# Unscaled tokens into the experts, and two modulation units moved ahead of them

## The chip, the core and the metric

The kernel runs on one core of one Trainium2 chip. The metric is the device time of one execution in microseconds; times of a kernel are given as the median of its runs. Engines are called by the profile's names: PE (TensorE, matrix products and transposes; PEld is its weight load), DVE (VectorE), ACT (ScalarE), POOL (GpSimd), SP (SyncE, which issues almost all DMAs; SPq is its queue).

## What is computed

256 tokens of width 1024 pass a first block and then two layers of a second block. The change touches the first block's mixture of experts and the second block's modulation:

```
x  = x + merged @ w_out                                  # first block, after attention and gMLP
h2 = rms_norm(x, norm2_g)                                # one scale per token, one gain per channel
gp = softmax(h2 @ rg_w + rg_b);  top-1 group of 4        # router
el = (h2 @ re_w + re_b) of that group's 8 experts; softmax, top-2, weights renormalised
y  = sum over 32 experts:  comb[:, e] * ((silu(h2 @ w_gate[e]) * (h2 @ w_up[e])) @ w_down[e])
x  = rms_norm(x + y, final_norm_g)
...
mod = silu(c) @ w_ada[l] + b_ada[l]                      # second block, for each layer l: shift, scale, gate
h   = rms_norm(x) * (1 + scale) + shift; RG-LRU and mLSTM branches; x = x + gate * (mix @ w_out_2[l])
```

All values are float32. Where a product needs precision, an operand is split into a high part rounded to the fp32r type and the remainder (`...h` and `...l` in the names), and three products replace one.

## The kernel before

Tokens lie in two tiles of 128 partitions (`i` = 0, 1), `x1[:, i, :]` with 1024 columns. The stretch that the change works on starts with the output projection of the first block, `out_proj` (L820), called at L960 with the four accumulators (token tile i, column half n); the last one, (1, 1), is cut in two pieces of 256 columns. Its last steps run accumulator by accumulator. Each finished accumulator goes to `fin1` (L939): DVE adds it to `x1` (L943), ACT squares it for the norm (`token_scale` L336, `meansq` L365), and POOL makes the norm scale `r2[:, i, 3:4]` (L373) once a token tile is complete.

The router follows: `r_transpose` (L892) transposes x1 on PE and copies it to `h2T` on DVE (L898), `r_logits` (L900) multiplies it with the router weights, `r_choice` (L909) is a chain of small DVE operations that ends in the mask `M` (L923) of each token's two experts, and `r_place` (L927) counts slots with a product of `M` and a triangle (L932). The dictionary `late` hangs the router's work for token tile 0 and the first half of tile 1 in front of steps of the projection. `r_tokens` (L884) makes the experts' input: ACT reads x1 with a step of eight columns, scales it by `r2`, and writes the high part `h2h` (L888); a second such ACT pass (L889) writes the scaled value in full, and DVE takes the difference `h2l` (L890).

Experts work in 16 pairs with 64 slots an expert. `Slots.half` (L982) builds a one-hot matrix `oht` of tokens against the 256 slots of two pairs on DVE, `gather` (matmuls at L1030) multiplies `h2h` and `h2l` with it, so that the slots' inputs `xg` come out transposed. A test of whether any expert has over 64 tokens (L1053, L1054) branches to a general path, which does not run with these inputs. `spread` (L242) copies token values along the partitions through a diagonal matrix made on POOL (L250) and a product (L252), into `bc` (L1103). For each pair, DVE picks each slot's weight out of `bc` (L1152), PE multiplies with gate and up weights (L1165), ACT takes the silu (L1169), DVE multiplies (L1170), and one pair later `down` (L1109) and `back` (L1128) apply the down weights and return the slots to the tokens. `eloads` (L486) issues the experts' weight chunks on SP's queue (1 MB of gate and up, or 1 MB of down), in a fixed order and as buffers come free.

A modulation unit, `ada_unit` (L393), loads 2 MB of `w_ada` as two tiles, multiplies them with silu(c) (L401, 16 rows of the profile for one unit), has ACT copy the result (L403) and later folds it into a column form (`ada_fold` L414, eight matmul rows at L421 for one unit, then DVE at L423 and L425). Layer 1's units (1, 0) to (1, 3) carry its shift and scale. Before the change (1, 0) stands at the start of the second block (L1275), and (1, 1), (1, 2) and (1, 3) are taken from the list `units` during layer 0's last part (L1559).

A scheduler sets the order of instructions on each engine, from the order written and a table of costs. `tc.keep_in_program_order` pins an instruction to its place among the pinned, and `tc.issue_after` forces an order behind another instruction. `warm` (L350) issues products whose result nobody reads.

## Time and profile before

| | before |
|---|---|
| median of 3 runs | 967.88 us (967.02 to 968.38) |
| profiled execution | 967.82 us, span 966.0 us |
| mean granted TensorE clock | 0.972 |
| PE busy | 908.2 us, 94% of the span |
| DVE, ACT, POOL busy | 597.6, 461.9, 22.6 us |

The span runs from the first to the last instruction; 1.8 us of the profiled execution lie outside it. In a timeline row the columns are start, busy time, engine, line, operation, output and inputs, shapes and count, and in brackets how long the engine had been idle before and what released it. A row with a count over 1 stands for several instructions in sequence, and its time runs over all of them. [...]

### The profile page before, as it was taken

To read this page: it belongs to the slowest core of one execution; us is meant where nothing else is said; L and a number is where in the kernel's file an instruction comes from. 1 tells how busy PE (TensorE), PEld (TensorE's weight loads), DVE (VectorE), ACT (ScalarE), POOL (GpSimd) and SP (SyncE) were. 2 spreads that over 40 slices of the span, in tenths; PEclk is the share of its full clock that TensorE was granted. 3 is DMA by queue.
4 is the path that set the end of the run, shared out by engine and by line. 5 is a ranking of instruction groups with operands and counts; after the bars stand their busy time and mean duration, and the time that the engine had idled before them with its cause. 6 is when DMAs were issued, how large, how long until landed. Compare 5 with 4: busy or idle time off the path is not lost.

```text
span 966.0 us, 15088 instructions
## 1 busy us (share of the span) xinstructions
PE 908.2 (94%) x5936; PEld 702.5 (73%) x5936; DVE 597.6 (62%) x1157; ACT 461.9 (48%) x806; POOL 22.6 (2%) x40
## 2 busy tenths in 40 slices
PE   7929998998899999999999999999999999999997
PEld 5928986997444445545448998897787999889776
DVE  5617773484366446445357979446756888935865
ACT  4513564353422112222136778565554678755742
POOL 1000000000100000000000000000100000000100
PEclk9968999998899999999999999999999999999999
DMA  9868479862798999999769753754627954574201
GB/s 317 247 116 287 131 238 360 324 221 79 268 356 328 401 400 400 403 399 404 265 226 310 235 175 131 256 180 143 228 88 242 281 187 163 172 264 174 88 1 44
DMA packets 135014, 230.22 MB, mean 238 GB/s; under 512 B 5784, under 2 KB 79512, under 8 KB 134936
## 3 DMA queue, kind: packets, MB, share of 16 engines
q1 hardware_dynamic: 132280, 227.00, 68.3%
q10 hardware_dynamic: 2656, 2.17, 0.7%
q8 instruction: 49, 0.80, 0.4%
q14 instruction: 29, 0.24, 0.1%
HBM read 226.53 MB, written 2.62 MB: 237 GB/s over the span
## 4 chain that ended last, share of the span: by engine, by line
PE 61%; DVE 4%; issue 3%; ACT 3%; POOL 1%; POOLq 0%; DVEq 0%; ACTq 0%
PE at L1165 11%; PE mm L272 10%; PE mm L271 10%; PE mm L270 10%; PE mm L1122 6%; PE mm L1135 3%; PE mm L1030 3%; PE mm L401 1%; PE mm L1397 1%; DVE wl L283 1%; PE at L1420 1%; ACT wh L282 1%; PE tp L1430 1%; PE at L271 0%; PE at L270 0%
## 5 line engine op out<-in xcount | busy, mean ns | idle before, releaser
L283 DVE TENSOR_TENSOR wl<-w,wh 128x1024 fp32r<-128x1024 f32 x164 | 199.1, 1218 | 122.1 <-ACT wh L282 120.5
L282 ACT ACTIVATE wh<-w 128x1024 fp32r<-128x1024 f32 x164 | 171.8, 1056 | 138.9 <-PE mm L271 76.4
L270 PE MATMUL mm<-hh,wh 128*128 128x256 f32 (+1 forms) x624 | 179.8, 288 | 3.9 <-ACT wh L282 3.3
L272 PE MATMUL mm<-hh,wl 128*128 128x256 f32 (+1 forms) x624 | 178.9, 288 | 0.8 <-DVE wl L283 0.8
L271 PE MATMUL mm<-hl,wh 128*128 128x256 f32 (+1 forms) x624 | 177.1, 284 | 0.9 <-DVE hl L563 0.9
L270 PEld LDWEIGHTS mm<-hh,wh 128*128 128x128 f32 (+1 forms) x624 | 119.4, 191 | 10.0 <-ACT wh L282 5.1
L1165 PE MATMUL at<-w,xg 128*64 128x512 f32 x512 | 122.9, 595 | 0.2 <-PEq L1054 0.2
L272 PEld LDWEIGHTS mm<-hh,wl 128*128 128x128 f32 (+1 forms) x624 | 119.2, 191 | 3.6 <-issue 1.7
L271 PEld LDWEIGHTS mm<-hl,wh 128*128 128x128 f32 (+1 forms) x624 | 119.2, 191 | 2.9 <-issue 1.5
L1165 PEld LDWEIGHTS at<-w,xg 128*64 128x64 f32 x512 | 38.9, 137 | 70.0 <-issue 65.9
L271 PE MATMUL mm<-wl,hh 128*128 128x256 f32 x256 | 72.1, 283 | 0.0
L272 PE MATMUL mm<-wh,hl 128*128 128x256 f32 x256 | 72.0, 283 | 0.0
L270 PE MATMUL mm<-wh,hh 128*128 128x256 f32 x256 | 71.6, 285 | 0.0
L1122 PE MATMUL mm<-w,heT 128*64 128x512 f32 x256 | 63.2, 598 | 0.0
L271 PEld LDWEIGHTS mm<-wl,hh 128*128 128x128 f32 x256 | 48.4, 189 | 2.7 <-issue 2.4
L270 PEld LDWEIGHTS mm<-wh,hh 128*128 128x128 f32 x256 | 47.6, 188 | 3.7 <-issue 2.0
L272 PEld LDWEIGHTS mm<-wh,hl 128*128 128x128 f32 x256 | 48.3, 189 | 1.7 <-issue 1.5
L1137 DVE TENSOR_TENSOR x<-x,mm 128x512 f32<-128x512 f32 x64 | 40.1, 680 | 14.8 <-PE mm L1135 14.8
L1170 DVE SCALAR_TENSOR_TENSOR sil<-at,wsl,sil 128x256 f32<-128x256 f32 x16 | 7.7, 483 | 66.9 <-ACT sil L1169 66.9
L1124 ACT ACTIVATE ys<-mm 128x512 fp32r<-128x512 f32 x32 | 19.1, 597 | 60.8 <-PE mm L1122 60.8
L1169 ACT ACTIVATE sil<-at 128x256 f32<-128x256 f32 x16 | 6.1, 383 | 79.2 <-PE at L1165 79.2
L1122 PEld LDWEIGHTS mm<-w,heT 128*64 128x64 f32 x256 | 18.7, 136 | 31.5 <-issue 28.7
(436 smaller groups left out, 1772.0 us busy)
## 6 DMA issues: line engine op xcount, KB each, us to landing
w<-in_w_in SPq DMA_DIRECT2D x55, 1024.0 KB, 7.5
w<-in_w_down SPq DMA_DIRECT2D x64, 512.0 KB, 10.3
w<-in_w_gate SPq DMA_DIRECT2D x60, 512.0 KB, 10.3
w<-in_w_up SPq DMA_DIRECT2D x60, 512.0 KB, 10.4
w<-in_w_ada SPq DMA_DIRECT2D x24, 1024.0 KB, 5.2
w<-in_w_out SPq DMA_DIRECT2D x20, 1024.0 KB, 5.0
w<-in_w_gate SPq DMA_DIRECT2D x8, 256.0 KB, 7.6
w<-in_w_up SPq DMA_DIRECT2D x8, 256.0 KB, 7.6
```

Of the source, the lines that this page charges most:

```text
L270: pin(TE.matmul(o, lhsT=lh, rhs=rh, start=start and k == 0, stop=False))
L271: pin(TE.matmul(o, lhsT=lh, rhs=rl, start=False, stop=False))
L272: pin(TE.matmul(o, lhsT=ll, rhs=rh, start=False, stop=stop and k == nk - 1))
L282: splits[S] = S.activation(out=h, in_=src, func=AF.Copy)
L283: splits[V] = V.tensor_tensor(out=l, in0=src, in1=f32(h), op=OP.subtract)
L401: r = TE.matmul(acc[32 * k:32 * k + 32, :], lhsT=cact[:, hf * 4 + k:hf * 4 + k + 1].to_broadcast([P, 32]), rhs=w[:, k * 512:(k + 1) * 512] ...
L1030: TE.matmul(ps[:, 256 * a:256 * a + 256], lhsT=part[i][:, k, :], rhs=oht[:, i, :], start=n == 0, stop=n == 3)
L1122: TE.matmul(po[64 * q:64 * q + 64, :], lhsT=heT[:, f * P + 64 * q:f * P + 64 * q + 64], rhs=wd[n][:, (2 * q + f) * 512:(2 * q + f + 1) * 5 ...
L1124: S.activation(out=y[:, 0, :], in_=po, func=AF.Copy)
L1135: r = TE.matmul(ps, lhsT=ohs[:, i * P:(i + 1) * P], rhs=y[:, part, :], start=part == 0, stop=part == 1)
L1137: V.tensor_tensor(out=xs, in0=xs, in1=ps, op=OP.add)
L1165: r = TE.matmul(gu[64 * q:64 * q + 64, :], lhsT=xg[:, k, o:o + CAP], rhs=w, start=k == 0, stop=k == KT - 1)
```

## The change

Five things change. (a) `r_tokens(i, n)` splits the unscaled x1, half a token tile at a time, right after that half was added: one ACT pass and one DVE subtraction over 512 columns, both reading x1 with a step of eight columns. The scaled copy is gone. (b) The norm scale is applied at the slots: a third `spread` brings `r2` into `bc[:, 4]`, one more DVE operation for each pair sums it over the slot's row into `wsl[:, 2:3]`, and the silu gets it as its scale; the other factor goes into the gate weight `gw`. (c) The units (1, 0) and (1, 1) are loaded while the first block's `w_out` is loaded and multiplied around the last router steps, and folded around the first gather. The later places take (1, 2) and (1, 3). (d) The slot count of token tile 0 is pinned between the accumulators (1, 0) and (1, 1), and four and then six `warm` products are pinned around the slot count of tile 1. (e) The general path's loads go to SP's queue, and no GpSimd DMA scratch is reserved.

```diff
-        def r_tokens(i, pool):
-            h2[i] = pool.tile([P, D], F32, tag=f"y{i}", name=nm("h2"))
...
-            S.activation(out=h2h[i], in_=x1k(i), func=AF.Copy, scale=r2[:, i, 3:4])
-            S.activation(out=h2k, in_=x1k(i), func=AF.Copy, scale=r2[:, i, 3:4])
-            V.tensor_tensor(out=h2l[i], in0=h2k, in1=f32(h2h[i][:]), op=OP.subtract)
+        def r_tokens(i, n):
+            c = slice(64 * n, 64 * n + 64)
+            split(h2h[i][:, :, c], h2l[i][:, :, c], x1k(i)[:, :, c])
...
             if (i, n) == (1, 0):
                 r_choice(0)
-                r_tokens(0, ro)
+            if not i:
+                r_tokens(0, n)
+            if i and n and c == 0:
+                r_tokens(1, 0)
             if i and n and c + w == 512:
-                r_transpose(1, 1)
-                rlast = r_logits(1, 1)
-                r_place(0)
+                pin = tc.keep_in_program_order
+                a = [psum(), psum()]
+                ada_mm(a[0], aws[0][0], 0, pin)
+                r_transpose(1, 1, True)
+                ada_mm(a[0], aws[0][1], 1, pin)
+                rlast = r_logits(1, 1, True)
+                for hf in range(2):
+                    ada_mm(a[1], aws[1][hf], hf, pin)
+                r_choice(1)
+                r_tokens(1, 1)
+                for j in range(2):
+                    ada_end(ro, *nexts.pop(0), a[j])
 
         late = {(6, 0, 1): lambda: [r_transpose(0, n, True) for n in range(2)],
                 (7, 0, 1): lambda: [r_logits(0, n, True) for n in range(2)],
+                (4, 1, 1): lambda: r_place(0, True),
...
+        def between():
+
+            if len(splits_done) == 3:
+                aws.extend(ada_load(*u) for u in nexts[:2])
+            splits_done.append(0)
...
         slots.half(0)
-        warm(6, rlast, h2h[0][:, 0:4, :])
-        r_choice(1)
-        last = r_place(1)
+        warm(4, rlast, h2h[0][:, 0:4, :], True)
+        last = r_place(1, True)
+        warm(6, rlast, h2h[0][:, 0:4, :], True)
...
+            V.tensor_tensor(out=gw, in0=gw, in1=r2[:, :, 3:4], op=OP.mult)
...
-                        G.dma_start(out=wf, in_=w[0, e].rearrange("(p k) c -> p k c", k=KT)[:, 2 * kq:2 * kq + 2, :])
+                        SY.dma_start(out=wf, in_=w[0, e].rearrange("(p k) c -> p k c", k=KT)[:, 2 * kq:2 * kq + 2, :])
...
-        bc = bp.tile([P, 4, T], F32, name="bc")
+        bc = bp.tile([P, 5, T], F32, name="bc")
...
+        pb = psum_t()
+        spread(bp, "sOH", r2[:, :, 3], pb[:, 0:256])
+        S.activation(out=bc[:, 4, :], in_=pb[:, 0:256], func=AF.Copy)
...
+            V.scalar_tensor_tensor(out=oa, in0=f32(ohs[:]), scalar=1.0, in1=bc[:, 4, :], op0=OP.mult, op1=OP.mult, accum_out=wsl[:, 2:3])
...
-            S.activation(out=sil, in_=gu[:, 0:256], func=AF.Silu)
+            S.activation(out=sil, in_=gu[:, 0:256], func=AF.Silu, scale=wsl[:, 2:3])
...
         with tc.issue_after(last.ins):
-            ada_unit(bp, 1, 0)
+            ada_unit(bp, *nexts.pop(0))
...
             if l == 0:
-                units += [(1, 1), (1, 2), (1, 3)]
+                units += nexts
...
-    nc = bacc.Bacc("TRN2", target_bir_lowering=False, num_devices=1)
+    nc = bacc.Bacc("TRN2", target_bir_lowering=False, num_devices=1, dynamic_dma_scratch_size=1024)
```

The order of instructions moves at three places. DVE, around the adds of the projection's results to x1 (`x`, L943 before, L955 after), before:

```order
L943 TENSOR_TENSOR x_66<-x_66,mm_1963 128x512
L943 TENSOR_TENSOR x_66<-x_66,mm_1964 128x512
L340 SCALAR_TENSOR_TENSOR r_1946<-r_1946 128x1
L898 COPY h2T<-tp_2106 128x512
L898 COPY h2T<-tp_2112 128x512
L911 SCALAR_TENSOR_TENSOR lg<-at_2121,r_1946,row_1942 128x36
L890 TENSOR_TENSOR h2l_2151<-h_293_2149,h2h_2150 128x1024
L912 TENSOR_REDUCE gmx_1948<-lg 128x1
L943 TENSOR_TENSOR x_66<-x_66,mm_1965 128x512
```

and with the change:

```order
L955 TENSOR_TENSOR x_66<-x_66,mm_1967 128x512
L283 TENSOR_TENSOR h2l_1965<-x_66,h2h_1963 128x8x64
L955 TENSOR_TENSOR x_66<-x_66,mm_1968 128x512
L340 SCALAR_TENSOR_TENSOR r_1946<-r_1946 128x1
L904 COPY h2T<-tp_2122 128x512
L283 TENSOR_TENSOR h2l_1965<-x_66,h2h_1963 128x8x64
L904 COPY h2T<-tp_2128 128x512
L917 SCALAR_TENSOR_TENSOR lg<-at_2137,r_1946,row_1942 128x36
L918 TENSOR_REDUCE gmx_1948<-lg 128x1
L919 SCALAR_TENSOR_TENSOR gat_1949<-lg,gmx_1948,cst 128x4
L955 TENSOR_TENSOR x_66<-x_66,mm_1969 128x512
```

The one remainder `h2l` of 1024 columns behind the logits has become two of 512 columns, of which one now stands between the two adds of tile 0 and one between the two copies that the logits need.

PE, from the end of the projection to the first gather (`at` takes the last piece, `M` is the mask, `cact` silu(c), `onesr` marks the slot counts' and warm products), before:

```order
L272 MATMUL at_1967<-wo_284_2062,ml 128x256
L895 MATMUL tp_2199<-cst,x_66 128x128 x4
L932 MATMUL at_2209<-M_1957,cst 128x32
L904 MATMUL at_2170<-vec,h2T 128x36 x4
L355 MATMUL tp_2266<-h2h_2150,onesr 128x512 x6
L1046 MATMUL tp_2368<-M_1957,onesr 128x32
L931 MATMUL at_2286<-M_1957,onesr 128x32
L932 MATMUL at_2286<-M_1957,cst 128x32
L1030 MATMUL mm_2316<-oht_2262,h2h_2150 128x256
```

and with the change:

```order
L272 MATMUL at_1971<-wo_284_2066,ml 128x256
L408 MATMUL mm_2218<-w_2072,cact 32x512 x4
L901 MATMUL tp_2224<-cst,x_66 128x128 x4
L408 MATMUL mm_2218<-w_2074,cact 32x512 x4
L910 MATMUL at_2187<-vec,h2T 128x36 x4
L408 MATMUL mm_2219<-w_2076,cact 32x512 x4
L408 MATMUL mm_2219<-w_2078,cact 32x512 x4
L355 MATMUL tp_2310<-h2h_1963,onesr 128x512 x4
L941 MATMUL at_2315<-M_1957,onesr 128x32
L942 MATMUL at_2315<-M_1957,cst 128x32
L355 MATMUL tp_2322<-h2h_1963,onesr 128x512 x6
L1062 MATMUL mm_2352<-oht_2306,h2h_1963 128x256
```

The slot count of tile 0 (`at_2209`) has left this place for one ahead of the last accumulator's products; two modulation units and four warm products have come in, and six warm products stand behind tile 1's slot count.

PE at the end of layer 0's output projection (`tp` and `at` of L1236 are the transposes of the next layer's first token tile, `xn`), before:

```order
L271 MATMUL mm_9641<-wo_9962,mh_9198 128x512
L401 MATMUL mm_9710<-w_9711,cact 32x512 x4
L401 MATMUL mm_9710<-w_9713,cact 32x512 x4
L272 MATMUL mm_9641<-wo_9961,ml_9199 128x512
L270 MATMUL mm_9642<-wh_9955,mh_9198 128x256
L401 MATMUL mm_9771<-w_9772,cact 32x512 x4
L401 MATMUL mm_9771<-w_9774,cact 32x512 x4
L271 MATMUL mm_9642<-wl_9956,mh_9198 128x256
L272 MATMUL mm_9642<-wh_9955,ml_9199 128x256
L421 MATMUL tp_9785<-cst,ada_9709 128x1 x4
L421 MATMUL tp_9832<-cst,ada_9770 128x1 x4
L1236 MATMUL tp_10030<-cst,xn_9635 128x128 x4
```

and with the change:

```order
L271 MATMUL mm_9718<-wo_9996,mh_9275 128x512
L272 MATMUL mm_9718<-wo_9995,ml_9276 128x512
L270 MATMUL mm_9719<-wh_9989,mh_9275 128x256
L271 MATMUL mm_9719<-wl_9990,mh_9275 128x256
L272 MATMUL mm_9719<-wh_9989,ml_9276 128x256
L1272 MATMUL tp_10064<-cst,xn_9712 128x128 x4
```

Both units and both folds are gone from this place.

## Rows read from the trace of the kernel before

**Rows 1.** The page: busy time of each engine, and the chain by engine.
```profile
PE 908.2 (94%) x5936; PEld 702.5 (73%) x5936; DVE 597.6 (62%) x1157; ACT 461.9 (48%) x806; POOL 22.6 (2%) x40
...
PE 61%; DVE 4%; issue 3%; ACT 3%; POOL 1%; POOLq 0%; DVEq 0%; ACTq 0%
```
**Rows 2.** Windows of the run: us, busy time (instructions) by engine, PEclk, DMA share, GB/s.
```profile
230.00:237.00 7.00, 6.71 (x30) 6.42 (x31) 3.40 (x15) 1.24 (x4) 0.00 (x0) 0.51 0.00 0
...
240.40:250.60 10.20, 6.65 (x27) 6.10 (x26) 6.78 (x37) 6.09 (x8) 0.00 (x0) 0.50 0.97 349
```
**Rows 3.** Timeline of PE from the projection's end to the first expert.
```profile
226.91 0.28 PE L272 MATMUL mm<-wh,ml 128*128 128x256 f32 x1
...
230.14 1.12 PE L895 MATMUL tp<-cst,x 128*128 128x128 f32 x4 [2.60 <-DVE x L943]
...
238.95 1.08 PE L904 MATMUL at<-vec,h2T 128*128 128x36 f32 x8 [0.64 <-DVE h2T L898]
239.87 2.49 PE L355 MATMUL tp<-h2h,onesr 128*128 128x512 f32 x6
...
246.60 0.64 PE L932 MATMUL at<-M,cst 128*128 128x32 f32 x2 [3.55 <-DVE M L923]
...
252.83 3.65 PE L1165 MATMUL at<-w,xg 128*64 128x512 f32 x16
```
**Rows 4.** Timeline of DVE in the same stretch.
```profile
221.45 0.69 DVE L943 TENSOR_TENSOR x<-x,mm 128x512 f32<-128x512 f32 x1 [2.03 <-PE mm L272]
222.99 0.16 DVE L340 SCALAR_TENSOR_TENSOR r<-r 128x1 f32<-128x1 f32 x1 [0.85 <-ACT jk L365]
...
228.20 1.22 DVE L890 TENSOR_TENSOR h2l<-h,h2h 128x1024 fp32r<-128x1024 f32 x1 [1.78 <-ACT h L889]
...
237.25 0.42 DVE L943 TENSOR_TENSOR x<-x,at 128x256 f32<-128x256 f32 x1 [1.24 <-PE at L272]
...
240.15 0.26 DVE L911 SCALAR_TENSOR_TENSOR lg<-at,r,row 128x36 f32<-128x36 f32 x1
...
244.36 1.22 DVE L890 TENSOR_TENSOR h2l<-h,h2h 128x1024 fp32r<-128x1024 f32 x1 [2.33 <-ACT h L889]
...
246.30 0.24 DVE L923 TENSOR_SCALAR M<-key,k 128x32 f32<-128x32 f32 x1
```
**Rows 5.** ACT: its strided pass (timeline), and contiguous passes of 1024 columns (page).
```profile
223.81 2.18 ACT L888 ACTIVATE h2h<-x,r 128x1024 fp32r<-128x1024 f32 x1 [0.85 <-POOL r L373]
...
L282 ACT ACTIVATE wh<-w 128x1024 fp32r<-128x1024 f32 x164 | 171.8, 1056 | 138.9 <-PE mm L271 76.4
```
**Rows 6.** Timelines of ACT and DVE at the start of the experts.
```profile
263.86 1.28 ACT L1169 ACT_TABLE_LOAD   x1
...
271.50 0.48 DVE L1152 SCALAR_TENSOR_TENSOR oa<-bc,cst 128x256 f32<-128x256 f32 x1
```
**Rows 7.** Windows of the experts' stretch (columns as in the second group).
```profile
256.00:315.00 59.00, 58.18 (x272) 25.31 (x270) 30.74 (x96) 14.71 (x34) 4.07 (x4) 1.00 0.94 339
315.00:460.00 145.00, 145.00 (x732) 70.37 (x729) 73.49 (x192) 30.84 (x80) 0.00 (x0) 1.00 1.04 401
```
**Rows 8.** What the experts' products at L1165 waited for (view of one line): us, times.
```profile
  DMA w<-in_w_gate: 1.1, 4
```
**Rows 9.** The branch on the count of tokens (view of line L1054): PE's wait, ns.
```profile
L1054 PEldq COMPARE_BRANCH  x1: 4734/4734/4734, 255.2 to 255.2; - x1
```
**Rows 10.** Timeline of all engines at the end of layer 0.
```profile
728.55 1.92 PE L401 MATMUL mm<-w,cact 128*32 128x512 f32 x16
...
729.24 0.72 ACT L1228 ACTIVATE xn<-x,scales 128x512 f32<-128x512 f32 x1 [0.85 <-POOL scales L373]
...
729.68 2.36 DVE L283 TENSOR_TENSOR wo<-w,wo 128x1024 fp32r<-128x1024 f32 x2
...
733.15 1.84 PE L421 MATMUL tp<-cst,ada 128*128 128x1 f32 x16
...
734.85 0.64 PE L1236 MATMUL tp<-cst,xn 128*128 128x128 f32 x4
```

More of the change, by code (lines that the diff above doesn't have):

```diff
@@ L348, in model, with warm @@
     heads = {}
-    def warm(n, after, x):
+    def warm(n, after, x, keep=False):
         pt = psum_t()
@@ L409, in ada_unit @@
             gates.append(a)
-        return r
     folds, gates = [], []
+    nexts = [(1, c) for c in range(4)]
     def ada_fold():
@@ L1007, in model @@
         with tc.issue_after(last.ins):
[L1008 to L1009 removed]
+            r_over(1)
             gw = small(1, "gw")
```

54 lines of the change are left out of this document (32 added, 22 removed).

## The prediction

> **What bounds the kernel now.** I read the page first: PE is busy for 94% of the span and carries 61% of the chain that ended last, no other engine over 5% [rows 1]. So a microsecond counts if it is PE's time or PE's wait. Then I looked, stage by stage, for the places where PE is not simply full. There are two, and the change touches both. Between the first block's projection and the first expert PE stands still or runs at half speed: the granted clock is 0.51 from 230 to 237 us and 0.50 from 240.4 to 250.6 us [rows 2], and the PE rows show idle times of 2.60, 0.64 and 3.55 us, each ended by DVE [rows 3]. At the end of layer 0 PE is full, but part of what fills it is modulation work in front of the transposes that the next layer waits for [rows 10]. The experts between are full of products: 145 of 145 us from 315 to 460 us [rows 7]. A shift of their start is a shift of the end.
>
> **Layer 0's end.** Two units (16 rows each; the second repeats the first's 1.92 us) and two folds (1.84 us together) stand ahead of the transposes of `xn` at 734.85 us [rows 10]. From 728.55 us, PE needs 6.3 us to get there; without units and folds the few products between them remain, 0.9 us, so PE would be ready 5.4 us earlier, at 729.45. But `xn` itself is only there at 729.24 + 0.72 = 729.96 us. So the transposes start at about 730.0 us: **4.85 us saved**. Bounds: 5.4 us if `xn` comes earlier too, 3.8 us if DVE, which at 729.68 starts 2.36 us of weight splits, comes to its part of the new head a microsecond too late. I take 4.85 since nothing shown makes `xn` earlier and the split moves forward with the loads it waits for.
>
> **Ahead of the experts, token tile 0.** The new pass on ACT covers half the columns of the 2.18 us row, which is twice the 1.06 us of a contiguous pass [rows 5]: 1.1 us a half. For DVE no strided row exists. Its contiguous subtraction over 1024 columns takes 1.22 us and an add over 512 takes 0.69 us [rows 4]; 0.69 us is the lower bound, and with ACT's ratio 1.42 us the upper. The one row has the engine, the other the access pattern, so I take the middle, 1.05 us.
>
> [...]
>
> Before, the add of half (0,1) at 221.45 us, the square behind it and `r` at 222.99 us led straight to the two copies [rows 4]. Now the first remainder pushes the add by 0.15 us, ACT's split of the second half stands before the square (1.1 us), and a remainder stands between the copies (1.05 us); 0.5 us of it is swallowed, because logits and copies had waited for PE. Logits end 1.8 us later, at 227.9 us.
>
> Then PE waits for the slot count of tile 0, now pinned ahead of the last accumulator. The chain from `lg` to `M` takes 246.54 - 240.15 = 6.4 us for tile 1, of which 2.33 + 1.22 us are ACT's second pass and the remainder [rows 4], so 2.85 us by itself; for tile 0, in which other short rows are left out of it, 2.7 us. With the add of (1,0), 0.69 us, and a remainder, 1.05 us, inside it, `M` is there at 232.3 us. PE, out of work 0.7 us after the logits, idles **3.7 us instead of 2.60** [rows 3]. Behind this the slot count and six products that used to run before the wait (up to 226.91 us) still come: 1.9 us at half clock. So what started at 230.14 us starts at 234.2. If the full clock returns where it did before, at 237.0 us [rows 2], the last 17 products take 0.12 us instead of 0.21, and the last add ends at about 239.8 us instead of 237.67; if not, at 241.7.
>
> **Token tile 1.** The last half now needs: square 0.6, ACT's split 1.1, remainder 1.05, copy 0.69, logits 0.95 us, because the remainder stands before the copy on DVE. Logits end at 244.2 us instead of 240.03. But the choice behind them runs without its stall: 2.85 us, `M` at 247.2 us instead of 246.54. In this time PE does one unit and a half and four warm products at no cost, provided the clock is full: the second unit is 1.85 us, warm products 0.21 us each (0.41 at half clock [rows 3]), done by 246.9 us.
>
> **From M to the first expert.** Before: 252.83 - 246.60 = 6.2 us, partly at half clock [rows 3]. Now in PE's order: slot count 0.3, six warm products 1.3, eight gather products 0.95, a fold 0.85, 24 gather products 2.8, a fold 0.85, together 7.1 us at full clock, so 254.4 us: **1.6 us later**. At half clock the work from the logits on costs up to 2 us more before it recovers. Before, the clock was half in all of this until 250.6 us after idle times like those I still expect; I take a third of it: the first expert **2.3 us later**. With remainders of 0.69 us it is 1.0, with 1.42 us 3.8 later. Below that: 1 us earlier, if the clock stays full throughout and no remainder delays a copy.
>
> **Start of the experts.** The first silu used to wait for PE alone. Now it waits for the third `spread` and for six DVE rows of about 0.48 us [rows 6] behind it, and an activation table load of 1.28 us [rows 6] comes behind ACT's evacuations of the second gather. PE has pair 1's products and the second gather to do meanwhile. I put 0.5 us here (0 if these cover it; 2.6 us if both the chain and the table load are seen). The 16 more DVE rows later are hidden: DVE is busy 73.5 of 145 us there [rows 7].
>
> **Transfers.** Four loads of 1 MB go ahead of chunks of experts' weights: 4 MB or 10.5 us at 401 GB/s. Up to 315 us the queue runs at 339 GB/s because buffers are full, which leaves 59 x 62 = 3.7 MB to catch up [rows 7]. About 1 us of lead is lost; PE waited for gate weights 1.1 us in all [rows 8]. I put 0 (up to 1 us). SP's jump over the general path's loads, now its own, has a bound in PE's 4.7 us at the same branch [rows 9]; the weights issued next are not the next ones needed. I put 0.
>
> **Sum**, against the profiled execution: 967.82 - 4.85 + 2.3 + 0.5 = 965.8 us. The median, 967.88 us, is 0.06 us above it, and I leave that out. With all bounds: 961.4 to 973.
>
> **Rivals.** First, *slower: half clock from the last logits to the gather*. PE still has two waits of 2 to 4 us ahead of this stretch, and after such waits the clock was granted at 0.50 for 10.2 us [rows 2]. Then the last add is at 241.7 us, and unit, warm products and the first third of the gather at double length cost 4 to 5 us more. The start is 7 us late: 967.82 - 4.85 + 7 + 0.5 = 970.5 us. It decides from a start 6.3 us late. Against it: the first unit and its products keep PE busy just where it idled. Second, *no change: the saving at layer 0's end is half hidden*, because DVE and ACT set the new head's pace: 2.5 us saved, 2.8 lost, 968.1 us. For it, DVE's 2.36 us of splits; against it, PE was full there and DVE had gaps. Third, *more gain: strided reads cost DVE nothing and the stall that leaves the choice is all gain*. Start unchanged, no early stall: 963.0 us. For it, 3.55 us of idle at `M` vanish; against it, PE has 6 us more work in this stretch.
>
> **How the numbers follow.** A measurement of this kernel tells about 0.2%, 1.9 us, from no change. My sum lies 2.1 us below the median, hardly over this bound. Chances: the sum as it stands, 964 to 967 us, 0.42; half hidden 0.20; more gain 0.20; half clock 0.18. Two thirds of the first and all of the third lie below 965.9 us: faster 0.46. Same: the rest of the first and most of the second, 0.34. Slower: the half clock and a little of the second, 0.20. The likeliest case has its own range, 964 to 967 us; for 8 in 10 I take in the more-gain case and the nearer part of the half clock: 962.3 to 970.0 us.
>
> **What would show it.** The transposes at the end of layer 0 some 5 us nearer to the rows before them, and no modulation rows there; PE's wait ahead of the slot count of tile 0 near 3.7 us; DVE's remainders at 1.05 us each; no idle at `M` of tile 1; the first expert product 2.3 us later than 252.83 us. Wrong if the first expert comes over 5 us late or before 252 us, if PE waits for weights in the experts by several microseconds, or if the head of layer 1 starts less than 3 us earlier against the experts' end.

## The result and the profile after: slower by 1.2%

The changed kernel takes 979.89 us (median of 4 runs, 977.51 to 982.33) beside 968.13 us of the kernel before. The ratio is 1.0121, interval 1.0097 to 1.0144. The forecast was 965.8 us with a range up to 970.0, and 0.20 on "slower". The profiled execution took 980.33 us, with a span of 978.6. One of the eight executions of e1_gpsimd below ran at a granted clock of 0.65 (1291.07 us) and is left out of its median and ratio.

The page of the changed kernel has the same picture as that of before [rows 1], and so doesn't say where 12 us went:

```profile
PE 911.8 (93%) x5942; PEld 701.1 (72%) x5942; DVE 607.5 (62%) x1194; ACT 456.9 (47%) x807; POOL 23.3 (2%) x42
...
PE 62%; DVE 4%; ACT 3%; issue 3%; POOL 1%; POOLq 0%; DVEq 0%; ACTq 0%
```

What tells it is the time of four points that both programs pass: the first expert product, the third pair's first gate product, the first transposes of `xn` at the head of layer 0 (behind the experts), and those at the head of layer 1. First the PE timeline of before, at the third pair:

```profile
274.58 0.38 PE L1114 MATMUL tp<-cst,sil 128*128 128x128 f32 x2
274.89 3.65 PE L1165 MATMUL at<-w,xg 128*64 128x512 f32 x16
```

and the PE timeline of the changed kernel, from the projection to the third pair:

```profile
233.12 0.64 PE L942 MATMUL at<-M,cst 128*128 128x32 f32 x2 [4.09 <-DVE M L929]
...
243.66 1.08 PE L910 MATMUL at<-vec,h2T 128*128 128x36 f32 x8 [1.29 <-DVE h2T L904]
...
248.30 0.41 PE L942 MATMUL at<-M,cst 128*128 128x32 f32 x2 [0.44 <-DVE M L929]
...
256.04 6.22 PE L1201 MATMUL at<-w,xg 128*64 128x512 f32 x26
264.20 1.08 PE L1201 MATMUL at<-w,xg 128*64 128x512 f32 x4 [1.93 <-PEq L1086]
269.08 0.80 PE L252 MATMUL tp<-dg,onesr 128*128 128x512 f32 x1 [3.80 <-POOL dg L250]
269.80 3.68 PE L1201 MATMUL at<-w,xg 128*64 128x512 f32 x6
...
289.59 0.44 PE L1149 MATMUL tp<-cst,sil 128*128 128x128 f32 x2 [1.26 <-DVE sil L1206]
289.96 2.37 PE L1201 MATMUL at<-w,xg 128*64 128x512 f32 x10
```

The first expert comes 256.04 - 252.83 = 3.2 us later. From there to the third pair it was 274.89 - 252.83 = 22.1 us and is now 289.96 - 256.04 = 33.9: **11.9 us lost in this one stretch**. The rest of the experts loses 1.5 us more: the transposes at the head of layer 0 are at 523.07 instead of 506.44 us. The end of layer 0 gives back 4.9 us, for those at the head of layer 1 are at 746.57 instead of 734.85 [rows 10]. Layer 1 adds 0.9 us, and 3.2 + 11.9 + 1.5 - 4.9 + 0.9 = 12.6 = 978.6 - 966.0 us. The timeline at layer 0's end:

```profile
745.78 0.72 ACT L1264 ACTIVATE xn<-x,scales 128x512 f32<-128x512 f32 x1 [0.86 <-POOL scales L375]
...
746.57 0.66 PE L1272 MATMUL tp<-cst,xn 128*128 128x128 f32 x4 [0.82 <-DVE xn L1266]
```

No unit stands there, and PE waits 0.82 us for `xn`.

In the stretch that failed, the rows that stand out are PE's waits of 1.93 us, ended by the branch over the general path (L1086), and of 3.80 us, ended by POOL. The six products behind them take 3.68 us; in the run e1 below, in which this second wait is gone, six products at the same place take 1.93 us. The granted clock, as a share of PE's full clock, was 0.73 from 265 to 270 us and 0.59 from 270 to 275: behind the start of the idle time it fell from 1.00 to 0.50, at which it was from 268 to 274 us (below: half clock). So the next view is that of the branch's line. Before (L1054; engine, operation, count: ns min/median/max, first and last start in us):

```profile
L1054 POOLq EVENT_SEMAPHORE  x4: 17/43/43, 253.0 to 253.2; - x4
...
L1054 POOLq COMPARE_BRANCH  x1: 45/45/45, 250.2 to 250.2; - x1
...
L1054 PEldq EVENT_SEMAPHORE  x1: 51/51/51, 260.0 to 260.0; - x1
```

and after (L1086):

```profile
L1086 SPq EVENT_SEMAPHORE  x8: 17/17/17, 264.7 to 267.8; - x8
L1086 POOLq COMPARE_BRANCH  x1: 45/45/45, 252.3 to 252.3; - x1
...
L1086 PEldq COMPARE_BRANCH  x1: 6346/6346/6346, 257.7 to 257.7; - x1
L1086 SPq COMPARE_BRANCH  x1: 45/45/45, 257.7 to 257.7; - x1
...
L1086 PEldq EVENT_SEMAPHORE  x1: 51/51/51, 264.1 to 264.1; - x1
```

In these rows a jump of POOL or SP is a branch, then nothing, then signals (EVENT_SEMAPHORE, four from POOL before, eight from SP after). I read them as those that the skipped path would have given. Before, POOL owned the path's loads: 250.2 to 253.0, a jump of 2.8 us, over long before PE's own at 260.0. After, SP owns them. It comes to the branch 5.4 us behind POOL, needs 7.0 us for the jump and 3.1 us for its eight signals, and ends at 267.8, 3.7 us behind PE. POOL's `dg` waits for them, since its tile takes turns with those of the skipped path (both have the tag `sOH`): it starts at 267.99 us, behind the last. PE's 3.80 us of idle are this wait and the 1.0 us that one `dg` takes.

Why SP's jump is long, the windows suggest (columns as in [rows 2]; PEclk is the granted clock, DMA the mean busy share of the 16 DMA engines). Before, in POOL's jump:

```profile
250.20:253.00 2.80, 2.80 (x23) 2.67 (x24) 1.79 (x10) 1.92 (x8) 0.00 (x0) 0.93 0.15 60
```

and after, in SP's:

```profile
257.70:264.70 7.00, 5.07 (x24) 1.51 (x20) 0.00 (x0) 1.28 (x1) 0.00 (x0) 1.00 1.05 396
```

The transfers nearly stood still in the one (share 0.15) and were full in the other (1.05). The two units that went ahead of the experts hold 4 MB of buffers until PE is through with them (244.67 + 1.92 = 246.6 us), so the experts' chunks that used to be loaded before the branch are loaded during it. This is also why SP is late: it issues its last two loads ahead of the branch at 255.09 and 256.79 us, by my reading as buffers come free. With the units back at their old place (e4 below) the last one is issued at 247.58 us.

### The profile page after: what moved, and what is told of

It reads as the page before. It is cut to its first block, busy times and chain, and to the rows that moved or that the text cites. A ratio compares the mean times of both kernels' runs of the same rounds, so it can differ in the third digit from the quotient of the medians.

```text
span 978.6 us, 15133 instructions
## 1 busy us (share of the span) xinstructions
PE 911.8 (93%) x5942; PEld 701.1 (72%) x5942; DVE 607.5 (62%) x1194; ACT 456.9 (47%) x807; POOL 23.3 (2%) x42
## 4 chain that ended last, share of the span: by engine, by line
PE 62%; DVE 4%; ACT 3%; issue 3%; POOL 1%; POOLq 0%; DVEq 0%; ACTq 0%
PE at L1201 12%; PE mm L272 10%; PE mm L270 10%; PE mm L271 10%; PE mm L1157 6%; PE mm L1170 3%; PE mm L1062 2%; PE mm L1433 1%; PE mm L408 1%; PE at L1456 1%; DVE wl L283 1%; ACT wh L282 1%; PE tp L1466 1%; PE tp L1149 1%; PE at L270 0%
## 5 line engine op out<-in xcount | busy, mean ns | idle before, releaser
L1201 PE MATMUL at<-w,xg 128*64 128x512 f32 x512 | 126.7, 601 | 1.9 <-PEq L1086 1.9
L1157 PE MATMUL mm<-w,heT 128*64 128x512 f32 x256 | 65.9, 600 | 0.0
L1205 ACT ACTIVATE sil<-at,wsl 128x256 f32<-128x256 f32 x16 | 7.6, 475 | 84.1 <-PE at L1201 82.2
L1157 PEld LDWEIGHTS mm<-w,heT 128*64 128x64 f32 x256 | 18.6, 136 | 30.9 <-issue 26.2
L1170 PEld LDWEIGHTS mm<-ys,ohs 128*128 128x128 f32 x128 | 22.3, 188 | 20.8 <-issue 13.8
## 6 DMA issues: line engine op xcount, KB each, us to landing
w<-in_w_gate SPq DMA_DIRECT2D x8, 256.0 KB, 7.6
w<-in_w_up SPq DMA_DIRECT2D x8, 256.0 KB, 7.3
```

Of the source, the lines that this page charges most:

```text
L1157: TE.matmul(po[64 * q:64 * q + 64, :], lhsT=heT[:, f * P + 64 * q:f * P + 64 * q + 64], rhs=wd[n][:, (2 * q + f) * 512:(2 * q + f + 1) * 5 ...
L1170: r = TE.matmul(ps, lhsT=ohs[:, i * P:(i + 1) * P], rhs=y[:, part, :], start=part == 0, stop=part == 1)
L1201: r = TE.matmul(gu[64 * q:64 * q + 64, :], lhsT=xg[:, k, o:o + CAP], rhs=w, start=k == 0, stop=k == KT - 1)
```

## The experiments

The texts that were put down before each run speak of three theories. A: SP's jump over its 384 loads holds POOL and through it PE. B: full transfers make every engine's jump slow. C: the third `spread` and the longer chain to the first silu cost the time. The pinned slot count and the order of products in the experts came up as further parts. What the runs leave is A and B together, with the pin and a share of C beside them. "First expert" is the time of the first expert product in the profile, "stretch" from there to the third pair's start. Before: 252.83 and 22.1 us; after: 256.04 and 33.9. Where sizes are compared between runs, a run's distance from before is its ratio less 1, times 968 us: 11.7 us for the change. The right columns come from the one profiled execution, which can lie some us off the median (g4: 977.45 beside 973.33 us, x1: 980.37 beside 977.19, f3: 967.01 beside 969.50).

| run | median us | ratio and interval | first expert | stretch |
|---|---|---|---|---|
| e1_gpsimd | 974.02 | 1.0074 (1.0049 to 1.0099) | 254.38 | 27.7 |
| e2_before_sync | 968.74 | 1.0012 (0.9994 to 1.0029) | 253.88 | 22.2 |
| e3_no_path | 971.39 | 1.0036 (1.0019 to 1.0053) | 259.29 | 23.4 |
| e4_units_back | 974.64 | 1.0071 (1.0051 to 1.0091) | 254.24 | 25.8 |
| f1_hold | 980.93 | 1.0141 (1.0124 to 1.0158) | 257.34 | 33.6 |
| f2_gp_hold | 976.62 | 1.0099 (1.0082 to 1.0116) | 256.38 | 27.9 |
| f3_place | 969.50 | 1.0030 (1.0017 to 1.0044) | 249.78 | 27.0 |
| f4_all | 971.80 | 1.0042 (1.0026 to 1.0057) | 249.06 | 29.9 |
| d1_fill | 965.33 | 0.9976 (0.9964 to 0.9987) | 255.25 | 22.0 |
| g4_place | 973.33 | 1.0060 (1.0037 to 1.0084) | 253.21 | 34.1 |
| g2_gp_place | 969.21 | 1.0013 (1.0002 to 1.0024) | 251.01 | 27.7 |
| g5_units_early | 971.13 | 1.0037 (1.0022 to 1.0052) | 253.48 | 25.2 |
| x1_no_slot_norm | 977.19 | 1.0091 (1.0064 to 1.0117) | 258.74 | 31.2 |
| x2_sp_late | 965.21 | 0.9972 (0.9958 to 0.9986) | 253.47 | 22.0 |
| x3_before_pins | 964.53 | 0.9961 (0.9946 to 0.9976) | 253.05 | (26.2) |
| x4_gp_place_pins | 964.71 | 0.9972 (0.9952 to 0.9992) | 253.34 | (32.1) |

The two values in brackets belong to another order of the products and are not to be compared with the others. From the third pair to the end of the experts the pairs' starts are the same distances apart, to 0.1 us, in the changed kernel, e1, f1, f2, f3, g2 and g4: what differs among these arises ahead of it.

### Is it the branch, and whose part of it?

**e1_gpsimd** gives the path's loads back to GpSimd and leaves the rest of the change (with 4 KB of scratch).

```diff
-                        SY.dma_start(out=wf, in_=w[0, e]...
+                        G.dma_start(out=wf, in_=w[0, e]...
...
-    nc = bacc.Bacc(..., dynamic_dma_scratch_size=1024)
+    nc = bacc.Bacc(..., dynamic_dma_scratch_size=4096)
```

> The changed kernel with the general path's loads issued by GpSimd again, with a smaller scratch than before. Theory A (SP's jump over its 384 loads, 257.7 to 267.8 us, holds DVE and POOL, and through them PE): SP signals at once, the 3.8 us wait of PE for the first diagonal matrix shrinks to under 1.5 us and the run is 3 to 7 us faster than the change, 973 to 977 us. Theory B (the transfer engines are full at the branch, DMA share over 1.0 where it was 0.13, and every engine's jump takes longer for that): GpSimd's jump takes as long as SP's did, and the time stays at 978 to 981 us. Theory C (the third spread and the longer chain to the first silu cost the early time): no change, 979 to 980 us, the branch waits moving without effect.

The distance falls from 11.7 to 7.2 us, the stretch from 33.9 to 27.7. `dg` no longer waits for SP. The PE timeline at this place:

```profile
262.39 1.08 PE L1201 MATMUL at<-w,xg 128*64 128x512 f32 x4 [1.78 <-PEq L1086]
...
263.99 1.93 PE L1201 MATMUL at<-w,xg 128*64 128x512 f32 x6
```

The idle time of 3.80 us is gone, and with it the half clock behind it (granted clock 1.00 from 250 to 280 us): the six products take 1.75 us less, and the two `spread` products among them 0.3 us less each. These are the 6.2 us. But the stretch is still 5.6 us longer than before. PE's own jump (6126 ns at 256.0) falls into full transfers as well, and PE waits 1.78 us at its end (0.20 before): 1.6 us. Of the rest 2.8 us belong to the norm at the slots (x1 below); 1.2 us are not placed.

**e2_before_sync** puts the same loads on SP in the kernel before.

```diff
-                        G.dma_start(out=wf, in_=w[0, e]...
+                        SY.dma_start(out=wf, in_=w[0, e]...
...
-    nc = bacc.Bacc(...)
+    nc = bacc.Bacc(..., dynamic_dma_scratch_size=1024)
```

> The kernel before with only the general path's loads moved to SP. Theory A: SP's jump now takes some 7 us plus 3 us of signals, DVE and POOL wait for it, the run is 3 to 7 us slower than before, 971 to 975 us. Theory B: at the branch the transfer engines are nearly idle (0.13), SP's jump takes 2 to 4 us as GpSimd's did (250.2 to 253.0), and the time is within 1.5 us of before, 967 to 970 us. Theory C: as before, 968 us.

No difference that can be measured. SP by itself isn't the cost: its jump takes 2.6 us there, and POOL's took 2.8 before.

**e3_no_path** leaves out the general path for too many tokens, and with it the branch, from the changed kernel.

```diff
-        over = nc.values_load(ovi[0:1, 0:1], min_val=0, max_val=2 * T)
-        with tc.If(over > CAP):
-            cw = bp.tile([P, 256], F32, tag="ohx", name="cw")...
...
```

> The changed kernel without the general path and its branch (left out: the path for over 64 tokens at one expert). Theories A and B: nobody jumps, the early stretch loses the 1.9 and 3.8 us of PE's idle time and most of the half clock after it, the run is 7 to 11 us faster than the change, 969 to 973 us. Theory C: the branch was not what mattered, at most 3 us faster, 977 us or more.

8.2 us of the 11.7 go with the path, and the stretch falls to 23.4 us. No other single edit of the change takes away as much. The first expert comes late in this profile (259.29 us): in it the clock was 0.50 from 230 to 240 us, and it took 973.56 us, 2.2 above the run's median.

**e4_units_back** keeps the change, but leaves both units where they were at layer 0's end.

```diff
-                a = [psum(), psum()]
-                ada_mm(a[0], aws[0][0], 0, pin)
...
-                aws.extend(ada_load(*u) for u in nexts[:2])
+                pass
```

> The changed kernel with the two modulation units back at their old places, so that their 4 MB are not loaded ahead of the experts' weights; the loads of the general path stay with SP. Theory B: the queue is empty again at the branch, jumps take 3 to 5 us, the second gather comes 5 to 9 us earlier, layer 0's end loses its 4.9 us: 972 to 977 us. Theory A: SP's jump costs the same 7 us, so only the 3 us of PE's work ahead of the experts come off and 4.9 us go on: 980 to 983 us. Theory C: 981 to 982 us for the same reason.

The distance falls by 4.8 us although the 4.9 us at layer 0's end are given up: ahead of the third pair the units cost about 10 us. SP now comes to the branch at 252.5, beside POOL's 252.2, and signals until 258.3, ahead of PE. Neither the loads on SP alone (e2) nor the change without the early units has the wait for SP. It takes both.

**d1_fill** asks whether full transfers make a jump long. It is e2 with 2 MB of loads that nobody needs, issued ahead of the branch.

```diff
         eloads(17)
+        fill = [bp.tile([P, 2048], F32, name=nm("fill")) for _ in range(2)]
+        for q, t in enumerate(fill):
+            tc.keep_in_program_order(SY.dma_start(out=t[:]..., in_=A["w_ada_2"][0]...))
```

> The kernel before with the general path's loads on SP, as in the second run, and 2 MB of extra loads that nobody reads issued behind the 17 chunks, so that the transfer engines stay full at the branch; nothing else. Theory B (a jump takes long when the transfers are full): SP's jump takes 4.5 to 7 us instead of 2.6, DVE's 4.5 to 6 instead of 3.0, the first expert comes when it did, the second gather 2.5 to 6 us later: 971 to 975 us. If a jump does not care about transfers: 968 to 969.7 us, the jumps as they were.

The lines of the branch in e2 (L1054):

```profile
L1054 SPq EVENT_SEMAPHORE  x8: 17/17/17, 253.4 to 253.9; - x8
L1054 SPq COMPARE_BRANCH  x1: 45/45/45, 250.8 to 250.8; - x1
```

and in d1 (L1057):

```profile
L1057 SPq EVENT_SEMAPHORE  x8: 17/17/17, 258.7 to 259.3; - x8
L1057 SPq COMPARE_BRANCH  x1: 45/45/45, 252.1 to 252.1; - x1
...
L1057 PEldq COMPARE_BRANCH  x1: 3393/3393/3393, 258.5 to 258.5; - x1
```

The windows of these two jumps, in e2:

```profile
250.80:253.40 2.60, 2.60 (x19) 2.60 (x18) 1.49 (x10) 1.25 (x5) 0.00 (x0) 0.74 0.10 36
```

and in d1:

```profile
252.10:258.70 6.60, 6.60 (x38) 4.23 (x38) 2.89 (x14) 2.29 (x8) 0.00 (x0) 0.88 0.88 325
```

Same engine, same path, same place in the program: 2.6 us at a share of 0.10, 6.6 at 0.88. On the jump theory B held. On the time it missed: the kernel isn't slower but 2.3 us faster than before. The jump cost nothing, because SP's signals, at 259.3 us, still come ahead of PE's own (258.5 + 3.4 = 261.9 us), and by then the extra loads were through. The gain is of another kind, below under x3.

How the end of the branch sets `dg`, in seven profiles:

| profile | SP's last signal | PE's jump ends | `dg` starts |
|---|---|---|---|
| after | 267.8 | 264.0 | 267.99 |
| g4_place | 265.7 | 261.2 | 265.87 |
| x1_no_slot_norm | 270.5 | 266.5 | 270.70 |
| e2_before_sync | 253.9 | 261.2 | 261.41 |
| d1_fill | 259.3 | 261.9 | 262.53 |
| e1_gpsimd | not on SP | 262.1 | 262.47 |
| f1_hold | 271.5 | 266.5 | 270.40 |

In the first six `dg` follows the later of the two (in d1 PE's own signal comes at 262.4, half a microsecond behind its jump's end). In f1 SP's eight signals are spread from 265.3 to 271.5 us, and the first `dg` starts 0.2 us behind the seventh (270.2): it waits for SP, but not for the last signal. In the changed kernel DVE's `ohx` (L1016) also ends just ahead of `dg`, at 267.95 us. It isn't the cause: in g4 it starts at 259.80, and `dg` still waits for SP; in e1 it starts at 265.92, behind `dg`. Three rows of `dg`, in the POOL timeline of g4:

```profile
265.87 3.03 POOL L250 TENSOR_TENSOR dg<-cst,sp 128x512 fp32r<-128x512 f32 x3 [26.93 <-SPq L1086]
```

in that of f1:

```profile
270.40 1.04 POOL L250 TENSOR_TENSOR dg<-cst,sp 128x512 fp32r<-128x512 f32 x1 [27.50 <-SPq L1086]
```

and in that of e2:

```profile
261.41 4.14 POOL L250 TENSOR_TENSOR dg<-cst,sp 128x512 fp32r<-128x512 f32 x4 [21.25 <-PEq L1054]
```

**Two attempts on the moment at which SP arrives** did not do what they were to do. **f1_hold** was to hold chunk loads back behind the branch (six fewer ahead of it):

```diff
-        eloads(17)
+        eloads(11)
```

> The changed kernel in which SP issues only 11 instead of 17 weight chunks ahead of the branch and the other six right behind it. The units stay moved, the general path's loads stay with SP. Theory B (the jump is slow because the transfers of these chunks fill the engines at that time): SP's jump shrinks from 7 to 2 to 4 us, PE's from 6.3 to 4 to 5, the second gather comes 6 to 9 us earlier after the first expert, 971 to 974 us. Theory A (SP's jump is slow by its length): 978 to 981 us. If the six later chunks come too late, PE waits for weights behind the second gather and the time is 975 to 985 us with that wait in the trace.

The planner put nine loads of 0.5 MB between SP's reading of the count and its branch all the same. SP came even later (258.9 us), signalled until 271.5, and PE's jump took 7.5 us. The time is that of the change.

**x2_sp_late** was to send SP late to the branch of d1, by six dummy loads into two tiles:

```diff
-        for q, t in enumerate(fill):
+        for q, t in enumerate(fill * 3):
```

> The run with filled transfers once more, but with six extra loads into the same two tiles, so that SP waits for the earlier ones to land and reaches its branch some 6 to 8 us later, at 258 to 260 us. If the moment decides, SP's signals end at 264 to 269 us, after PE's own jump, the first diagonal matrix on POOL waits for them, and the time is 2 to 8 us above the run with filled transfers, 967.5 to 973 us. If only the length of the jump matters, as there: 964.5 to 966.5 us.

Four of the six went behind the branch, and SP came to it at 250.6 us, as before. It says nothing on lateness; its jump took 7.4 us in filled transfers. A direct hold of SP alone was not achieved. That lateness counts beside slowness rests on d1 and e4, in which SP is slow (6.6 and 5.2 us) but comes to the branch with POOL, and costs nothing; an SP that is late but quick was not run.

**f2_gp_hold** is f1 with the path's loads on GpSimd:

```diff
-        eloads(17)
+        eloads(11)
...
-                        SY.dma_start(out=wf, in_=w[0, e]...
+                        G.dma_start(out=wf, in_=w[0, e]...
```

> The same hold with the general path's loads on GpSimd. Theory B: the other engines' jumps shrink too, 2 to 4 us faster than the run with GpSimd's loads alone, 970 to 972.5 us, and about as fast as the hold with SP's loads, since in an idle queue it doesn't matter who jumps. Theory A: 973.5 to 975 us, as with GpSimd's loads alone.

It has both sorts of jump in one profile: POOL's, at 252.6, takes 2.6 us (share 0.43), PE's, at 258.0, 7.2 us in full transfers. Nothing is gained over e1; the time lies above both ranges that were expected.

### The pinned slot count of tile 0

**f3_place** (on f2), **g4_place** (on the change) and **g2_gp_place** (on e1) take the pin away and issue the slot count behind the last accumulator, as before the change. The edit is the same in all:

```diff
                 pin = tc.keep_in_program_order
+                r_place(0)
...
-                (4, 1, 1): lambda: r_place(0, True),
```

> As the run before, with the slot count of tile 0 behind the last accumulator again, not pinned ahead of it. If that pin costs what I read (PE's idle 4.09 us ahead of it against 2.60 before, with six products and the slot count behind the wait), the first expert comes 1.5 to 3 us earlier and the time is 967.5 to 970 us. If DVE's remainders alone set the pace, under 1 us of gain.

> The changed kernel with one edit, the slot count of tile 0 back behind the last accumulator. The pin's price as the pair of runs with GpSimd's loads showed it is 7 us; if it is the same here, 971.5 to 974.5 us, the first expert 5 to 7 us earlier, and the stretch from there to the second gather still some 34 us because the jumps are what they were. If the two runs differed by anything else, under 3 us.

> Slot count unpinned and the general path's loads on GpSimd, no hold of chunks. If the two effects add (5.7 and 7 us), 966 to 968.5 us, which is level with before; the first expert near 250 us and the stretch to the second gather near 28 us.

The distance falls by 6.7 us (f2 to f3), 5.9 (after to g4) and 5.9 (e1 to g2). The PE timeline of e1 at this place:

```profile
231.31 0.64 PE L942 MATMUL at<-M,cst 128*128 128x32 f32 x2 [4.09 <-DVE M L929]
```

and that of g2:

```profile
235.36 0.41 PE L942 MATMUL at<-M,cst 128*128 128x32 f32 x2 [0.74 <-DVE x L955]
```

The wait for `M` is gone, and the accumulator's products run in it. In g4 the stretch stays long (34.1 us) with SP's wait in it: the two costs are separate ones. How much earlier the first expert comes differs more from profile to profile (2.8 us from after to g4, 3.4 from e1 to g2, 6.6 from f2 to f3) than the times do, and the clock goes with it: from 230 to 235 us it was 0.50 in g4, 0.97 in g2 and 1.00 in f3, and 0.50 in all three with the pin. The rows agree: a product of 128x256 takes 0.41 us there in g4, e1 and f2, and 0.28 us in g2 and f3. So part of the pin's price seems to be the half clock behind PE's idle 4 us. The clock can be at half there without the pin too: g4's profile shows it, and is the slowest of its four executions. No run took the two parts from each other.

**f4_all** leaves out of f3 the six warm products (they compute nothing) and puts the folds at the fifth pair.

```diff
-        warm(6, rlast, h2h[0][:, 0:4, :], True)
...
-        while folds:
-            ada_fold()
...
+            while pair == 4 and folds:
+                ada_fold()
```

> As the run before, without the six warm products behind tile 1's slot count and with the two folds in the fifth pair instead of the first gather. PE's rows between the mask and the first expert lose 1.4 and 1.7 us, of which the folds' 1.7 come back later in full PE time: 1 to 2 us faster than the run before if the clock stays full, 966 to 968.5 us; no gain or 1 us slower if the clock falls to half in the gather without the warm products.

The first expert comes 0.7 us earlier, but PE's jump takes 8.0 us and the time is no better. What was won ahead of the branch was lost in it.

**g5_units_early** puts the units' products ahead of the last accumulator, so that their buffers come free earlier and the chunks are loaded before the branch.

```diff
+                (4, 1, 1): lambda: units_early(),
...
+        def units_early():
+            for ws in aws:
+                accs.append(psum())
+                for hf in range(2):
+                    ada_mm(accs[-1], ws[hf], hf, tc.keep_in_program_order)
```

> As the run before, with the two units' products moved ahead of the last accumulator, some 10 us earlier, so that their four weight buffers come free before the chunks need them. Theory B: the chunks that were late now load from 230 us on, the transfers are empty at the branch as before the change, jumps shrink to 3 to 5 us, the stretch to the second gather to 23 to 25 us: 963 to 966 us. If the units' 3.7 us of products only delay the last accumulator, or the buffers were not what held the chunks: 967 to 970 us.

The mechanism shows: transfers are at 0.98 and 1.00 from 230 to 240 and from 240 to 250 us, PE's jump falls from 6.2 to 3.5 us, the stretch from 27.7 to 25.2. But the products now stand on the way to the choice, and the first expert comes 2.5 us later; in this profile the clock was also at 0.54 from 240 to 250 us (0.99 in g2 from 230 to 250), so that the delay is not the products' alone. The time is 2.3 us above that of g2, and above both ranges that were expected.

### The norm at the slots

**x1_no_slot_norm** leaves out the third spread, the added row on DVE and the factor in the silu.

```diff
-            V.scalar_tensor_tensor(out=oa, in0=f32(ohs[:]), ..., in1=bc[:, 4, :], ..., accum_out=wsl[:, 2:3])
...
-            S.activation(out=sil, in_=gu[:, 0:256], func=AF.Silu, scale=wsl[:, 2:3])
+            S.activation(out=sil, in_=gu[:, 0:256], func=AF.Silu)
```

> The changed kernel without the third spread, without the added DVE row of each pair and with an unscaled silu (left out: the norm scale inside the silu). If the norm at the slots is what is left of the early loss, the wait of PE ahead of the second gather and for the first silu (0.63, 0.48 and 1.26 us) go, and 16 added rows of 0.42 us on DVE: 1.5 to 4 us faster than the change, 976 to 978.4 us. If those waits only hide others, 979 to 980.5 us.

The stretch is 2.7 us shorter, with SP's wait still in it (signals until 270.5 us). The rows place it: from the second `spread` of tile 1 to the third pair's first transposes it is 5.1 us here and 7.9 us in the changed kernel, e1 and g2. In the changed kernel PE waits 0.63 us for `dg` and 1.26 us for `sil` there. By the times the distance falls by 2.9 us, with intervals that overlap. So the chain of the norm is worth some 2.7 us, the upper bound of the forecast's own step (2.6), and isn't the main loss.

### The order in the experts

d1 and x2 were faster than before without a reason in the stretch. From the sixth pair's start to the ninth's the distances are 16.5, 12.7 and 16.5 us in both, and 17.9, 16.3 and 16.6 us before; behind that 12.7 and 16.5 in turn in before and d1. **x3_before_pins** keeps all pairs' gate and down products of the kernel before in program order.

```diff
-                        TE.matmul(po[64 * q:64 * q + 64, :], ...)
+                        tc.keep_in_program_order(TE.matmul(po[64 * q:64 * q + 64, :], ...))
...
-                    if pair < 2 and k + q:
+                    if pair > 1 or k + q:
                         tc.keep_in_program_order(r)
```

> The kernel before with all pairs' products at the gate and up weights and at the down weights kept in program order, nothing else. If pairs 5 to 7 are slow (17.9, 16.3 and 16.6 us, against 12.7 and 16.5 in turn later) because products that use one half of the array stand next to others of the same half, they now take 12.7 to 16.5 us and the time falls by 3 to 6 us, 962 to 965 us. If it is something else, within 1.5 us of before.

**x4_gp_place_pins** has the same pins on g2.

> The best version so far of the changed kernel (slot count unpinned, general path's loads on GpSimd) with the same pins. If the order of half-array products is what its pairs 3 to 8 lose, 963.5 to 966.5 us, faster than both kernels; if not, 968 to 970 us.

Both beat both kernels: x3 by 3.8 us against before, x4 by 2.7; against g2 x4 gains 4.0 us. The PE timeline of before, at the seam of two pairs:

```profile
318.87 2.13 PE L1135 MATMUL mm<-ys,ohs 128*128 128x512 f32 x8
320.94 1.07 PE L1165 MATMUL at<-w,xg 128*64 128x512 f32 x2
321.94 0.44 PE L1114 MATMUL tp<-cst,sil 128*128 128x128 f32 x2
```

and of x3:

```profile
316.05 2.13 PE L1135 MATMUL mm<-ys,ohs 128*128 128x512 f32 x8
318.02 0.38 PE L1114 MATMUL tp<-cst,sil 128*128 128x128 f32 x2
318.33 3.65 PE L1122 MATMUL mm<-w,heT 128*64 128x512 f32 x16
321.81 7.04 PE L1165 MATMUL at<-w,xg 128*64 128x512 f32 x32
```

The profile gives these products as 128*64, those at L1135 as 128*128. In a block they start in twos: 32 take 7.04 us, 0.44 for two. At the seam of before two run one behind the other, 1.0 us. In the starts of the products, 28 of 768 before have no partner that starts within 0.06 us of them, and 16 in x3: six such seams less, an estimated 3.4 us at 1.0 - 0.44 us each, of the 4.3 us by which the stretch from the first expert to the head is shorter (249.3 instead of 253.6 us). In d1 there are 20. PE is "busy" for 145 of 145 us (315 to 460) in either kernel. The changed kernel has 28 too.

## Why the prediction was wrong

**Right.** *Layer 0's end*: 4.85 us forecast, 4.9 measured, and the reason given (the transposes wait for `xn`) stands in the row. *Ahead of the experts*: 2.3 us forecast, 3.2 measured. The DVE and ACT timelines of the changed kernel have the terms. DVE's rows:

```profile
221.61 0.69 DVE L955 TENSOR_TENSOR x<-x,mm 128x512 f32<-128x512 f32 x1
...
224.23 1.08 DVE L283 TENSOR_TENSOR h2l<-x,h2h 128x512 fp32r<-128x512 f32 x1 [0.32 <-ACT h2h L282]
...
239.83 0.42 DVE L955 TENSOR_TENSOR x<-x,at 128x256 f32<-128x256 f32 x1 [0.21 <-PE at L272]
...
248.01 0.24 DVE L929 TENSOR_SCALAR M<-key,k 128x32 f32<-128x32 f32 x1
```

and ACT's row:

```profile
223.02 1.18 ACT L282 ACTIVATE h2h<-x 128x512 fp32r<-128x512 f32 x1
```

A remainder takes 1.07 to 1.14 us (1.05 forecast), half a pass 1.11 to 1.18 (1.1), the wait ahead of the slot count 4.09 us (3.7). The last add ends at 240.25 us (239.8), tile 1's logits at 244.7 (244.2), `M` is there at 248.25 (247.2).

*The clock*: the rival "half clock" fell, and with it the place at which I looked for a loss. The changed kernel's windows:

```profile
230.00:237.00 7.00, 3.73 (x17) 3.44 (x17) 4.19 (x18) 1.59 (x3) 0.00 (x0) 0.53 0.00 0
237.00:250.00 13.00, 11.27 (x81) 7.21 (x82) 7.26 (x30) 5.09 (x12) 0.54 (x1) 1.00 0.59 203
```

The granted clock is full from 237 us on; before it was half up to 250.6 us [rows 2]. The forecast had put 0.7 us of its 2.3 on half clock here, which this profile does not have. Without it the sum is 1.6 us, and the measured 3.2 us come from `M` (1.0 us later than forecast) and from the products behind it (7.7 us from the slot count to the first expert, 7.1 forecast). That 2.3 comes near 3.2 is in part luck. The clock was not full in every execution either: in the profiles of e3 and x1 it is 0.50 from 230 to 240 us (products of 128x256 take 0.41 us in x1), and their first expert comes at 259.29 and 258.74 us.

The signs that the forecast named for itself came out, but for an idle time of 0.44 us at `M`, and none of those that were to show it wrong did. They were all looked for ahead of the first expert, in weights and at layer 0's end; none looked at the branch.

**Wrong: "Transfers", and with it "Start of the experts".** The sentence that failed is the one on SP's jump: "has a bound in PE's 4.7 us at the same branch [rows 9]; the weights issued next are not the next ones needed. I put 0." It has three errors. It asked who waits for SP's next loads, and not who waits for the signals that SP gives for the skipped path: POOL's `dg` does, and PE behind it. It took PE's 4.7 us for a bound on a jump; with full transfers SP's is 5 to 8 us. And it had the 4 MB of the moved units as lost lead of weights ("about 1 us"), which is right as far as it goes (the experts' first products wait 0.9 us for gate weights, before 1.1 [rows 8]), but did not see that they push the chunks' loads into the time of the branch. Put at 0.5 us in all, and that for the norm's chain to the first silu, this stretch measured 11.9. With the path's loads off SP 6.2 of them are gone (e1), with chunks loaded before the branch 2.5 more (g2 to g5, PE's jump 3.5 instead of 6.2 us), and 2.7 belong to the norm at the slots (x1), where the forecast's upper bound was 2.6: 11.4 together, if they add up, which no run tried. Of the 6.2 us some 3.8 are PE's idle time and some 2.3 the half clock behind it, by the rows of the changed kernel and e1.

**Only half seen: the pinned slot count.** The forecast had the wait in its sum, and the sum held. But that this pin alone is worth 6 to 7 us, and that without it the first expert can come earlier than before (251.01 us in g2, 249.78 in f3, though 253.21 in g4's profile; 252.83 before), it did not work out.

The range failed for the same reason: its upper bounds took in half the clock and DVE's rows, but for the branch a bound of 0.

**Still open.** The rows give an estimate for lateness against slowness: had SP come with POOL at 252.3 us, even its 10.1 us of jump and signals would have ended at 262.4; had it come at 257.7 but needed e2's 3.1 us, at 260.8; PE's own jump ended at 264.0. Either alone would have been hidden. No run shows the second case. Open too are the price of the pin without the clock, the 1.5 us later in the experts and 0.9 us in layer 1. With the branch mended, the pin removed and the products pinned (x4) the change stands where before stands with the same pins (x3): the 4.9 us at layer 0's end are paid for ahead of the experts.

## What to carry to other kernels

A path that never runs had a price here, 8.2 of the 11.7 us (e3): ask for every engine when it comes to the branch, how full the transfers are then, and who waits for the signals behind its jump. With the loads moved from POOL's queue to SP's, these signals ended at 267.8 us instead of 253.2, behind what SP does first. And the 4 MB that were moved ahead of this stretch cost about 10 us ahead of the third pair (e4): they held buffers up to 246.6 us, and by my reading the chunks that waited for these were loaded at another moment. Last, a forecast's own signs should cover each stretch that it puts at nothing.

## What the runs showed of the hardware

In these runs a jump of SP or POOL over this path takes 2.5 to 2.8 us at a transfers' share of 0.10 to 0.44, and 5.2 to 8.0 us at 0.76 to 1.05. Eight of the jumps (the time from branch to first signal, the transfers' share in just this window):

| jump | share | us |
|---|---|---|
| e2, SP | 0.10 | 2.6 |
| before, POOL | 0.15 | 2.8 |
| f2, POOL | 0.43 | 2.6 |
| e4, SP | 0.80 | 5.2 |
| d1, SP | 0.88 | 6.6 |
| e1, POOL | 0.98 | 5.7 |
| after, SP | 1.05 | 7.0 |
| g4, SP | 1.04 | 8.0 |

The other runs agree: 2.5 us in x3, f3 and f4 (share 0.12, 0.42 and 0.44), 5.2 to 7.4 us in f1, g2, g5, x1, x2 and x4 (0.76 to 1.04). Not every engine's jump has this price: ACT's signal comes 0.6 to 0.7 us behind its branch in every profile with the branch (255.2 and 255.8 us in the changed kernel).

The queues' view of the changed kernel shows packets of the kind "instruction", with a share of the same 16 engines; at the branch, from 250 to 268 us (queue, kind: packets, MB, share of 16 engines):

```profile
q1 hardware_dynamic: 2110, 5.78, 87.5%
q8 instruction: 2, 0.03, 0.7%
q14 instruction: 5, 0.04, 0.6%
```

and in as many microseconds of straight code, from 300 to 318 us:

```profile
q1 hardware_dynamic: 1925, 5.54, 81.1%
q8 instruction: 1, 0.02, 0.4%
```

The same seven packets stand in e2's and d1's views from 250 to 262 us. That the price grows with the other transfers is shown by the runs (2.6 us in e2, 6.6 in d1). What makes a jump longer when they are full, and whether these packets have a part in it, isn't shown: no run took the packets away.
